# Attention by pairs of heads in the token mixer of a decoder layer: two column halves for the value product, feature-major output, probabilities divided on GpSimd

## The chip, the cores and the metric

The kernel runs on one core of a Trainium2 chip. The metric is the device time of one execution in microseconds (us), as the median over runs; lower is better. The profile and the trace come from one further execution.

## What is computed

One decoder layer on 512 tokens with D = 1024: a feed-forward block, a token mixer, a second feed-forward block and a gated per-layer embedding. The change lies in the mixer, which has two branches on the same input: a gated delta rule (8 heads of 64, chunks of 64 tokens, one triangular system per chunk and head) and sparse attention (8 heads of 64, the top 128 earlier keys of each query). Cut to what matters here:

```
def gated_delta_rule(q, k, v, g, beta):
    ...
    a_mat = jnp.where(strict, beta[..., :, None] * kk * decay, 0.0) + jnp.eye(C, dtype=jnp.float32)
    rhs = jnp.concatenate([v * beta[..., None], k * (beta * jnp.exp(gc))[..., None]], axis=-1)
    sol = lax.linalg.triangular_solve(a_mat, rhs, left_side=True, lower=True, unit_diagonal=True)
    ...

def dsa_attention(q, k, v, q_idx, k_idx, w_idx):
        ...
        _, sel = lax.top_k(score, top)
        valid = sel <= qpos[None, :, None]
        k_sel = gather(k, sel)
        v_sel = gather(v, sel)
        att = jnp.einsum("bqhd,bqkhd->bhqk", qb, k_sel).astype(jnp.float32) * (Dh ** -0.5)
        att = jnp.where(valid[:, None], att, -jnp.inf)
        prob = jax.nn.softmax(att, axis=-1).astype(v.dtype)
        return jnp.einsum("bhqk,bqkhd->bqhd", prob, v_sel)

def token_mixer(...):
    ...
    y_a = o_a.reshape(B, S, W_A) @ w_br_a
    ...
    o_b = dsa_attention(qb, kb, vb, qi, ki, w_i)
    y_b = o_b.reshape(B, S, W_B) @ w_br_b
    merged = jax.nn.sigmoid(g_a) * y_a + jax.nn.sigmoid(g_b) * y_b
    return merged @ w_out
```

## The kernel before

All large products take both operands as two exact parts and run three matmuls (lines 95 to 97). Weights are loaded in chunks of 128x2048 halves (`raw`), split by ACT (line 90) and DVE (line 91) ahead of use. The instructions are scheduled by the tile framework, which sets each engine's order from its own model of their times; inside an engine the order is fixed after that, and an instruction that waits holds back all behind it. PSUM has eight banks in two rings of four, `mmp` and `axp`.

**Attention.** There are no gathers: a bias tile per query tile `tt` (128 queries, S = 128 (tt + 1) keys) shuts out the keys that are not selected. 32 units (query tile, head) go through three steps, written one unit apart in the program. `att_soft`: one matmul of 64 rows gives the scores `pat` (line 705), DVE adds the bias and takes the minimum in one instruction (line 709, with a small read of the accumulator behind it), ACT takes the exponential and its sum (line 711), DVE the reciprocal (line 713). `att_tr`: the tile `at` is transposed 128 keys at a time into `ppt` (the helper of line 103) and copied to `pt` (line 725, DVE for heads 0 and 4, otherwise ACT). `att_pv`: per 128 keys a matmul with `pt` as weights and 64 columns of values moving gives `pob`, token-major (line 735); ACT writes it to `obt`, times the reciprocal of the sum (line 737). At the end 16 transposes `pobt` turn `obt` feature-major, and ACT and DVE make its parts `ob_hi` and `ob_lo` (lines 785, 786), which the branch's output product `pyb` uses.

**The delta rule beside it.** `chunk_blocks` gives the products k k and q k of four heads a step, times a decay tile `DT`: DMA, a select on POOL (line 638), subtraction on DVE, exponential on ACT, matmuls `pA`, and four products on DVE into `BT` and `KQs` (line 656). Its last three steps are written among the first units of the attention, behind units 2, 4 and 6, and at unit 7 `solve` follows: the diagonal blocks go out by DMA (`dgd`, line 661) and come back as `dz` (line 742). Then 31 steps of two DVE instructions each (lines 748 and 750) invert them in place. The result goes through memory again (`zd`, `dz`, `BT`, lines 752 to 758) and one DVE transpose makes `XC` (line 759). The 32x32 matmuls `pw` (line 820) need it, and so does the rest of the branch.

**What PE has besides.** `ptm` is the gate projection of the delta rule: 192 matmuls of 256 columns in the stretch looked at, which depend on neither the attention nor the solve. The tiles `at`, `DT` and the indexer's `rl` share a ring of three buffers, `pt` has two.

Of the kernel before, what the change touches and what calls it, by code (L numbers as in the profile page):

```python
# [7 lines left out]
F32 = mybir.dt.float32  # L8
# [7 lines left out]
T = 512  # L16
# [16 lines left out]
def layer_kernel(ctx, tc, x, pT, wf1, wo1, wfm, wsm, wtm, wbr, wout, wf2, wo2, wgate, wproj,  # L33
# [80 lines left out]
    def inv_rms(ss, half):  # L114
        """1/sqrt(mean + eps) from sums of squares over D, times 1/2 if half."""
# [7 lines left out]
    def first_u(tt, h, u, t):  # L123
        """make_u with the gain of FFN 1, which lies along the partitions."""
# [21 lines left out]
    def make_u(tt, h, gn, u, t):  # L146
        """u = rmsnorm(h) of one token tile, features on partitions, as two exact parts."""
# [70 lines left out]
    def start_tiles(tiles, u):  # L218
        """tiles: (weights, rows, evacuate), one half of the tokens after the other."""
# [316 lines left out]
    for tt in (3, 2, 1):  # L536
        S = 128 * (tt + 1)
        sc = tp.tile([128, S], F32, name=f"sc{tt}")
        for hd in range(8):
# [3 lines left out]
            rl = tp.tile([128, T], F32, name="rl", tag="at", bufs=3)  # L543
# [82 lines left out]
    def chunk_blocks():  # L626
        """Products k k and q k of one chunk of 128 tokens with the decay between two tokens, four heads a step."""
        for c in range(4):
# [6 lines left out]
            for h4 in range(2):  # L635
                DT = tp.tile([128, 4, 128], F32, name="DT", tag="at", bufs=3)
# [60 lines left out]
    units = [(tt, 2 * p + i) for p in range(4) for tt in (3, 0, 2, 1) for i in range(2)]  # L697
    ats, pts, pos, rss = {}, {}, {}, {}

    def att_soft(i):  # L700
        tt, hd = units[i]
        S = 128 * (tt + 1)
        b, pr = 64 * (hd % 2), hd // 2
        pa = axp("pat")
        PE.matmul(pa[:, :S], qbT[b:b + 64, pr, tt * 128:tt * 128 + 128], kbT[b:b + 64, pr, :S],  # L705
                  start=True, stop=True)
        at = tp.tile([128, T], F32, name="at", bufs=3)
        nm = sp.tile([128, 1], F32, name="nm", bufs=4)
        V.tensor_tensor_reduce(at[:, :S], pa[:, :S], bias[tt], 1.0, BIG, ALU.add, ALU.min, nm)
        sm1 = sp.tile([128, 1], F32, name="sm1", bufs=4)  # L710
        A.activation(at[:, :S], at[:, :S], AF.Exp, bias=nm, scale=-1.0, accum_out=sm1)
        rs = sp.tile([128, 1], F32, name="rs", bufs=6)
        V.reciprocal(rs, sm1)
        ats[i] = at
        rss[i] = rs

    def att_tr(i):
        tt, hd = units[i]
        S = 128 * (tt + 1)
        at = ats.pop(i)  # L720
        ppt = axp("ppt")
        for s_ in range(tt + 1):
            tr(ppt[:, s_ * 128:(s_ + 1) * 128], at[:, s_ * 128:(s_ + 1) * 128])
        pt = tp.tile([128, T], F32, name="pt", bufs=2)
        (A.copy if hd % 4 else V.tensor_copy)(pt[:, :S], ppt[:, :S])
        pts[i] = pt

    def att_pv(i):
        tt, hd = units[i]
        if hd % 2 == 0:  # L730
            pos[0] = mmp("pob")
        po, pt = pos[0], pts.pop(i)
        c = slice(64 * (hd % 2), 64 * (hd % 2) + 64)
        for s_ in range(tt + 1):
# [378 lines left out]
```

## Time and profile before

| what | value |
| --- | --- |
| median of 3 runs | 1319.71 us (1318.6 to 1321.0) |
| profiled execution, span of the trace | 1315.2 us |
| PE busy | 1291.6 us (98%) |
| DVE, ACT, POOL busy | 637.5, 469.0, 68.8 us |

The span is that of the trace's first to last instruction; the runs' times lie 4.5 us above it (1319.71 less 1315.2), and sums are made against the span and then carried to the median. Busy PE counts records; a float32 matmul of the attention leaves two records, a transpose one. Weight loads (PEld) run beside matmuls.

### The profile page before, as it was taken

To read this page: it belongs to the slowest core of one execution; us is meant where nothing else is said; L and a number is where in the kernel's file an instruction comes from. 1 tells how busy PE (TensorE), PEld (TensorE's weight loads), DVE (VectorE), ACT (ScalarE), POOL (GpSimd) and SP (SyncE) were. 2 spreads that over 40 slices of the span, in tenths; PEclk is the share of its full clock that TensorE was granted. 3 is DMA by queue.
4 is the path that set the end of the run, shared out by engine and by line. 5 is a ranking of instruction groups with operands and counts; after the bars stand their busy time and mean duration, and the time that the engine had idled before them with its cause. 6 is when DMAs were issued, how large, how long until landed. Compare 5 with 4: busy or idle time off the path is not lost.

```text
span 1315.2 us, 17630 instructions
## 1 busy us (share of the span) xinstructions
PE 1291.6 (98%) x7141; PEld 1095.4 (83%) x7141; DVE 637.5 (48%) x1088; ACT 469.0 (36%) x781; POOL 68.8 (5%) x71
## 2 busy tenths in 40 slices
PE   7999999999999999999999999989999999999997
PEld 6988888888889999887679888879888888888886
DVE  6233333322362699977685454563333333223555
ACT  6222222212252553445564223343222222212353
POOL 0000000000010000030001001220000000000000
PEclk9999999999999999999999999999999999999999
DMA  6233333333442223344305545522433333333331
GB/s 219 64 128 96 96 97 98 97 94 96 129 136 83 73 70 115 96 117 134 89 1 135 188 144 171 185 70 88 128 96 96 96 97 96 96 97 102 106 113 64
DMA packets 57777, 141.33 MB, mean 107 GB/s; under 512 B 17568, under 2 KB 20064, under 8 KB 57696
## 3 DMA queue, kind: packets, MB, share of 16 engines
q1 hardware_dynamic: 56688, 136.54, 34.0%
q10 hardware_dynamic: 1008, 3.67, 0.9%
q8 instruction: 56, 0.92, 0.3%
q14 instruction: 25, 0.20, 0.1%
HBM read 128.62 MB, written 11.57 MB: 107 GB/s over the span
## 4 chain that ended last, share of the span: by engine, by line
PE 88%; DMA 4%; DVE 4%; ACT 2%; POOL 1%; issue 1%; SPq 0%; POOLq 0%; DVEq 0%; ACTq 0%
PE pgu L95 11%; PE pgu L96 11%; PE pgu L97 11%; PE acc L95 6%; PE acc L97 6%; PE acc L96 6%; PE p L96 2%; PE p L97 2%; PE p L95 2%; PE ptm L97 2%; PE ptm L96 2%; PE ptm L95 2%; PE pg L95 2%; PE pg L97 2%; PE pg L96 2%; PE pat L705 2%
## 5 line engine op out<-in xcount | busy, mean ns | idle before, releaser
L91 DVE TENSOR_TENSOR wlo<-raw,whi 128x1024 fp32r<-128x1024 f32 x180 | 221.9, 1233 | 338.8 <-ACT whi L90 333.2
L90 ACT CAST whi<-raw 128x1024 fp32r<-128x1024 f32 x180 | 189.3, 1052 | 526.2 <-PE pgu L96 161.6
L96 PE MATMUL pgu<-ulo,whi 128*128 128x512 f32 x624 | 242.8, 389 | 0.0
L95 PE MATMUL pgu<-uhi,whi 128*128 128x512 f32 x624 | 242.8, 389 | 0.0
L97 PE MATMUL pgu<-uhi,wlo 128*128 128x512 f32 x624 | 242.8, 389 | 0.0
L97 PEld LDWEIGHTS pgu<-uhi,wlo 128*128 128x128 f32 x624 | 117.1, 188 | 24.5
L95 PEld LDWEIGHTS pgu<-uhi,whi 128*128 128x128 f32 x624 | 117.1, 188 | 24.2
L96 PEld LDWEIGHTS pgu<-ulo,whi 128*128 128x128 f32 x624 | 117.1, 188 | 24.1
L96 PE MATMUL acc<-wlo,hid 128*128 128x512 f32 x288 | 113.9, 395 | 0.0
L95 PE MATMUL acc<-whi,hid 128*128 128x512 f32 x288 | 113.9, 395 | 0.0
L97 PE MATMUL acc<-whi,hid 128*128 128x512 f32 x288 | 113.3, 396 | 0.0
L257 DVE TENSOR_TENSOR gt<-pgu,gt 128x512 f32<-128x512 f32 x39 | 27.0, 692 | 132.1 <-PE pgu L97 132.1
L96 PE MATMUL ptm<-wlo,uhi 128*128 128x256 f32 x256 | 72.1, 284 | 0.0
L97 PE MATMUL ptm<-whi,ulo 128*128 128x256 f32 x256 | 72.0, 284 | 0.0
L95 PE MATMUL ptm<-whi,uhi 128*128 128x256 f32 x256 | 71.7, 284 | 0.0
L96 PEld LDWEIGHTS acc<-wlo,hid 128*128 128x128 f32 x288 | 54.1, 188 | 13.1
L97 PEld LDWEIGHTS acc<-whi,hid 128*128 128x128 f32 x288 | 54.1, 188 | 13.1
L95 PEld LDWEIGHTS acc<-whi,hid 128*128 128x128 f32 x288 | 54.1, 188 | 13.0
L77 POOL TENSOR_TENSOR rinv<-ms,mhalf 128x1 f32<-128x1 f32 x32 | 19.0, 594 | 838.2 <-DVE ms L118 835.3
L97 PEld LDWEIGHTS ptm<-whi,ulo 128*128 128x128 f32 x256 | 48.9, 191 | 0.2
L96 PEld LDWEIGHTS ptm<-wlo,uhi 128*128 128x128 f32 x256 | 48.9, 191 | 0.1
L95 PEld LDWEIGHTS ptm<-whi,uhi 128*128 128x128 f32 x256 | 48.5, 191 | 0.2
(388 smaller groups left out, 2329.4 us busy)
## 6 DMA issues: line engine op xcount, KB each, us to landing
raw<-wf SPq DMA_DIRECT2D x88, 512.0 KB, 3.6
raw<-wo SPq DMA_DIRECT2D x44, 512.0 KB, 3.5
raw<-wfm SPq DMA_DIRECT2D x28, 512.0 KB, 3.7
raw<-wtm SPq DMA_DIRECT2D x20, 512.0 KB, 3.6
gd<-gst SPq DMA_DIRECT2D x16, 256.0 KB, 2.1
raw<-wbr SPq DMA_DIRECT2D x8, 512.0 KB, 3.8
grl<-gd SPq DMA_DIRECT2D x16, 256.0 KB, 3.1
raw<-wout SPq DMA_DIRECT2D x8, 512.0 KB, 4.1
```

The costliest lines, as they stand in the source:

```text
L77: G.tensor_tensor(out_, in_, e, op=ALU.pow)
L90: A.copy(hi[:, :n], raw[:, :n])
L91: (eng or V).tensor_sub(lo[:, :n], raw[:, :n], hi[:, :n].bitcast(F32))
L95: PE.matmul(ps, l[0], r[0], start=start, stop=False)
L96: PE.matmul(ps, l[0], r[1], start=False, stop=False)
L97: PE.matmul(ps, l[1], r[0], start=False, stop=stop)
L257: V.tensor_tensor(t[:, n], ps[:, n], t[:, n], op=ALU.mult)
L705: PE.matmul(pa[:, :S], qbT[b:b + 64, pr, tt * 128:tt * 128 + 128], kbT[b:b + 64, pr, :S], start=True, stop=True)
```

## The change

The units become 16 pairs (two heads of one row pair, one query tile). The two score matmuls of a pair are issued one behind the other in the two row halves of the array. After the reciprocal, POOL multiplies `at` by it in place (line 717 of the changed file), so that the transposes take normalized probabilities. The value product has the values as weights, 64 columns of the array for each head of the pair, and `pt` moving, so `pob` comes out feature-major, one bank for a pair's four query tiles. One ACT instruction per four pairs writes `obt` (line 743). The 16 transposes `pobt` are gone; `ob_hi` and `ob_lo` are made from `obt` in SBUF (lines 786 and 787). The ring of `at`, `DT` and `rl` has five buffers, that of `pt` four. The steps of `chunk_blocks` and the solve are written behind pairs 1, 2 and 3. Lines of the changed file are some two to seven higher than before.

```diff
-            rl = tp.tile([128, T], F32, name="rl", tag="at", bufs=3)
+            rl = tp.tile([128, T], F32, name="rl", tag="at", bufs=5)
...
-                DT = tp.tile([128, 4, 128], F32, name="DT", tag="at", bufs=3)
+                DT = tp.tile([128, 4, 128], F32, name="DT", tag="at", bufs=5)
...
-    units = [(tt, 2 * p + i) for p in range(4) for tt in (3, 0, 2, 1) for i in range(2)]
+    pairs = [(p, tt) for p in range(4) for tt in (3, 0, 2, 1)]
...
+    def att_soft(g):
+        p, tt = pairs[g]
         S = 128 * (tt + 1)
+        pa = [axp("pat") for _ in range(2)]
+        for i in range(2):
+            hb = slice(64 * i, 64 * i + 64)
+            PE.matmul(pa[i][:, :S], qbT[hb, p, tt * 128:tt * 128 + 128], kbT[hb, p, :S], start=True, stop=True)
+        ats[g] = []
+        for i in range(2):
+            at = tp.tile([128, T], F32, name="at", bufs=5)
...
+            V.reciprocal(rs, sm1)
+            G.tensor_scalar(at[:, :S], at[:, :S], rs, None, op0=ALU.mult)
+            ats[g].append(at)
...
+            pt = tp.tile([128, T], F32, name="pt", bufs=4)
+            (A.copy if (2 * p + i) % 4 else V.tensor_copy)(pt[:, :S], ppt[:, :S])
...
+    def att_pv(g):
+        p, tt = pairs[g]
+        if g % 4 == 0:
+            pos[0] = mmp("pob")
+        po, pt = pos[0], pts.pop(g)
         for s_ in range(tt + 1):
-            PE.matmul(po[:, c], pt[:, s_ * 128:(s_ + 1) * 128], vb[:, s_, hd * 64:(hd + 1) * 64],
-                      start=s_ == 0, stop=s_ == tt)
-        A.activation(obt[:, tt, hd * 64:hd * 64 + 64], po[:, c], AF.Copy, scale=rss.pop(i))
+            for i in range(2):
+                PE.matmul(po[64 * i:64 * i + 64, tt * 128:tt * 128 + 128], vb[:, s_, p * 128 + 64 * i:p * 128 + 64 * i + 64],
+                          pt[i][:, s_ * 128:(s_ + 1) * 128], start=s_ == 0, stop=s_ == tt, tile_position=(0, 64 * i))
+        if g % 4 == 3:
+            A.activation(obt[:, p, :], po, AF.Copy, scale=0.5)
...
-    for i in range(len(units) + 3):
-        if i < len(units):
-            att_soft(i)
-        if i in (2, 4, 6):
+    for g in range(len(pairs) + 2):
+        if g < len(pairs):
+            att_soft(g)
+        if g in (1, 2, 3):
             next(blocks, None)
-        if i == 7:
+        if g == 3:
             for _ in blocks:
                 pass
             ZC, XC, Z = solve()
...
-    for tt in range(4):
-        tk = slice(tt * 128, tt * 128 + 128)
-        pt = axp("pobt")
-        for pr in range(4):
-            tr(pt[:, pr * 128:pr * 128 + 128], obt[:, tt, pr * 128:pr * 128 + 128])
-        pt = pt.rearrange("p (a b) -> p a b", b=128)
-        A.activation(ob_hi[:, :, tk], pt, AF.Copy, scale=0.5)
-        V.scalar_tensor_tensor(ob_lo[:, :, tk], pt, 0.5, ob_hi[:, :, tk].bitcast(F32), op0=ALU.mult, op1=ALU.subtract)
+    for p in range(4):
+        A.copy(ob_hi[:, p], obt[:, p])
+        V.tensor_sub(ob_lo[:, p], obt[:, p], ob_hi[:, p].bitcast(F32))
```

What the change moves on the engines is read from the order of the instructions in the two programs. First DVE around the end of the solve (lines 748 and 750, in the changed file 754 and 756), before:

```order
L786 SCALAR_TENSOR_TENSOR ob<-pobt,ob 128x4x128
L748 TENSOR_TENSOR ztmp<-dz 128x60
L750 TENSOR_TENSOR dz<-dz,ztmp 128x30x2
L748 TENSOR_TENSOR ztmp<-dz 128x31
L750 TENSOR_TENSOR dz<-dz,ztmp 128x31
L91 TENSOR_TENSOR wlo<-raw,whi 128x1024 x2
L759 STREAM_TRANSPOSE dz<-dz 128x1024
```

and of the change (L712 is the add and minimum of a score tile, L716 the reciprocal, L787 makes `ob_lo`):

```order
L756 TENSOR_TENSOR dz<-dz,ztmp 128x30x2
L712 ISA at,nm<-pat,sc_3293 128x384
L712 ISA nm 128x1
L754 TENSOR_TENSOR ztmp<-dz 128x31
L712 ISA at,nm<-pat,sc_3293 128x384
L712 ISA nm 128x1
L756 TENSOR_TENSOR dz<-dz,ztmp 128x31
L716 RECIPROCAL rs<-sm_5880 128x1
L716 RECIPROCAL rs<-sm_5888 128x1
L712 ISA at,nm<-pat,sc_3345 128x256
L712 ISA nm 128x1
L787 TENSOR_TENSOR ob<-obt,ob 128x512 x2
```

Before, the last score tile is taken well ahead of the solve's last steps, and all four instructions that make `ob_lo` stand inside the solve. Now the score tiles of the last two pairs stand at and behind the solve's last step, and `ob_lo` behind that. Between the first and the last instruction of the solve stand 17 instructions on score tiles in both programs, and the same four copies of `pt`.

Next PE at the first `pw`, before:

```order
L97 MATMUL ptm<-whi,ulo 128x256
L820 MATMUL pw<-dz,BT 32x32 x64
L95 MATMUL pyb<-ob,whi 128x512
L96 MATMUL pyb<-ob,whi 128x512
L97 MATMUL pyb<-ob,wlo 128x512
```

and of the change:

```order
L95 MATMUL ptm<-whi,uhi 128x256
L96 MATMUL ptm<-wlo,uhi 128x256
L97 MATMUL ptm<-whi,ulo 128x256
L821 MATMUL pw<-dz,BT 32x32 x5
L740 MATMUL pob<-pt,vb 64x128 x3
L821 MATMUL pw<-dz,BT 32x32 x48
L95 MATMUL ptm<-whi,uhi 128x256
```

Before, all 192 `ptm` stand ahead of the first `pw`. Now 72 stand ahead of it and 120 behind, most of them before the first `pyb`. Of the 72, 14 stand ahead of the last pair's score matmuls, 10 between these and the transposes of the last but one pair, and 48 behind those, with 10 transposes and 7 value matmuls of the last two pairs.

Last POOL, of the change (before, only the select of `DT` stood here; the multiplications are line 717):

```order
L812 MEMSET S_5981 128x512
L717 TENSOR_SCALAR at<-at,rs 128x512 x2
L717 TENSOR_SCALAR at<-at,rs 128x128 x2
L638 AFFINE_SELECT DT<-DT 128x512
L717 TENSOR_SCALAR at<-at,rs 128x384 x2
L638 AFFINE_SELECT DT<-DT 128x512
L717 TENSOR_SCALAR at<-at,rs 128x256 x2
L638 AFFINE_SELECT DT<-DT 128x512
L717 TENSOR_SCALAR at<-at,rs 128x512 x2
```

The 32 multiplications come one for each score tile, the first eight between the selects of the last three steps of `chunk_blocks`; 16 of them belong to pairs whose score tiles stand inside the solve on DVE.

## Rows read from the trace of the kernel before

**Rows 1.** The page: engines, granted clock in 40 slices, shares of the chain.
```profile
PE 1291.6 (98%) x7141; PEld 1095.4 (83%) x7141; DVE 637.5 (48%) x1088; ACT 469.0 (36%) x781; POOL 68.8 (5%) x71
...
PEclk9999999999999999999999999999999999999999
...
PE 88%; DMA 4%; DVE 4%; ACT 2%; POOL 1%; issue 1%; SPq 0%; POOLq 0%; DVEq 0%; ACTq 0%
```
**Rows 2.** Windows: busy us and instructions of PE, PEld, DVE, ACT, POOL.
```profile
652.20:691.84 39.64, 39.59 (x258) 29.95 (x257) 32.67 (x122) 25.23 (x78) 0.00 (x0) 1.00 0.00 1
691.84:707.96 16.12, 16.12 (x139) 15.99 (x139) 4.01 (x4) 4.95 (x8) 3.85 (x3) 1.00 0.85 164
707.96:760.00 52.04, 52.04 (x596) 45.18 (x596) 30.83 (x57) 17.51 (x32) 3.17 (x2) 1.00 0.55 179
```
**Rows 3.** Groups of PE by form, 600 to 708: busy us, mean ns.
```profile
L735 PE MATMUL pob<-vb,pt 128*128 128x64 f32 x160 | 22.1, 276 | 0.0
```
**Rows 4.** Timeline of PE: start, duration, line, records; at 609, 675, 681, 707.
```profile
609.21 1.13 PE L705 MATMUL pat<-hz 64*128 64x512 f32 x4
...
675.71 0.91 PE L705 MATMUL pat<-hz 64*128 64x384 f32 x2
...
677.44 1.33 PE L735 MATMUL pob<-vb,pt 128*128 128x64 f32 x10
...
681.54 0.93 PE L103 MATMUL pobt<-cst,obt 128*128 128x128 f32 x7
...
707.08 0.28 PE L95 MATMUL ptm<-whi,uhi 128*128 128x256 f32 x1
707.20 0.28 PE L96 MATMUL ptm<-wlo,uhi 128*128 128x256 f32 x1
...
707.89 2.21 PE L820 MATMUL pw<-dz,BT 32*32 32x32 f32 x128
```
**Rows 5.** Groups of DVE, 652.20 to 691.84: busy us, mean ns, idle before, releaser.
```profile
L750 DVE TENSOR_TENSOR dz<-dz,ztmp 128x31 f32<-128x31 f32 (+15 forms) x31 | 10.5, 339 | 0.4
L748 DVE TENSOR_TENSOR ztmp<-dz 128x31 f32<-128x31 f32 (+15 forms) x31 | 10.5, 338 | 1.6 <-DMA dz<-dgd 1.2
L709 DVE CUSTOM_DVE_ANT_0 at<-pat,sc 128x256 f32<-128x256 f32 (+2 forms) x13 | 7.1, 546 | 2.7 <-PE pat L705 2.5
L713 DVE RECIPROCAL rs<-sm 128x1 f32<-128x1 f32 x18 | 2.9, 158 | 0.6 <-ACT at L711 0.4
L786 DVE SCALAR_TENSOR_TENSOR ob<-pobt,ob 128x512 fp32r<-128x512 f32 x4 | 2.8, 689 | 1.1 <-ACT ob L785 0.9
```
**Rows 6.** Timelines of DVE and SP at the solve's start and end.
```profile
644.87 2.58 SPq L661 DMA_DIRECT2D dgd<-BT  x4
...
652.21 0.19 DVE L748 TENSOR_TENSOR ztmp<-dz 128x31 f32<-128x31 f32 x1 [1.20 <-DMA dz<-dgd]
...
691.62 0.22 DVE L750 TENSOR_TENSOR dz<-dz,ztmp 128x31 f32<-128x31 f32 x1
...
700.39 1.25 DVE L759 STREAM_TRANSPOSE dz<-dz 128x1024 f32<-128x1024 f32 x1 [1.33 <-DMA dz<-zd]
```
**Rows 7.** Groups of POOL, 600 to 708 us.
```profile
L933 POOL TENSOR_TENSOR zs<-zs,prm 128x512 f32<-128x512 f32 x3 | 3.8, 1294 | 61.0 <-ACT zs L931 61.0
L638 POOL TENSOR_SCALAR_AFFINE_SELECT DT<-DT 128x512 f32<-128x512 f32 x5 | 3.2, 638 | 43.8 <-DMA DT<-rowd 43.8
```
**Rows 8.** Timelines of DVE and POOL near 817 us, and of DVE at 707 us.
```profile
817.95 2.32 DVE L91 TENSOR_TENSOR wlo<-raw,whi 128x1024 fp32r<-128x1024 f32 x1
...
817.51 1.68 POOL L975 TENSOR_TENSOR grl<-grl,ybm 128x512 f32<-128x512 f32 x1 [1.27 <-DVE grl L974]
...
707.64 1.23 DVE L91 TENSOR_TENSOR wlo<-raw,whi 128x1024 fp32r<-128x1024 f32 x1 [6.00 <-ACT whi L90]
```

**Rows 9.** Timeline of PE at the start of the span.
```profile
15.09 0.41 PE L96 MATMUL p<-ulo,whi 128*128 128x256 f32 x1
15.30 0.41 PE L97 MATMUL p<-uhi,wlo 128*128 128x256 f32 x1
```

More of the change, by code (lines that the diff above doesn't have):

```diff
@@ L696, in layer_kernel @@
     obt = mx.tile([128, 4, T], F32, name="obt", tag="oa")
-    units = [(tt, 2 * p + i) for p in range(4) for tt in (3, 0, 2, 1) for i in range(2)]
-    ats, pts, pos, rss = {}, {}, {}, {}
-    def att_soft(i):
-        tt, hd = units[i]
+    pairs = [(p, tt) for p in range(4) for tt in (3, 0, 2, 1)]
+    ats, pts, pos = {}, {}, {}
+    def att_soft(g):
+        p, tt = pairs[g]
         S = 128 * (tt + 1)
[L703 to L715, printed above, removed]
@@ L717, in att_tr @@
-    def att_tr(i):
-        tt, hd = units[i]
-        S = 128 * (tt + 1)
-        at = ats.pop(i)
-        ppt = axp("ppt")
-        for s_ in range(tt + 1):
[L723 to L734, printed above, removed]
-            PE.matmul(po[:, c], pt[:, s_ * 128:(s_ + 1) * 128], vb[:, s_, hd * 64:(hd + 1) * 64],
-                      start=s_ == 0, stop=s_ == tt)
-        A.activation(obt[:, tt, hd * 64:hd * 64 + 64], po[:, c], AF.Copy, scale=rss.pop(i))
+        pa = [axp("pat") for _ in range(2)]
@@ new lines, in att_soft @@
+        for i in range(2):
[4 more added lines that the diff above has]
+            at = tp.tile([128, T], F32, name="at", bufs=5)
+            nm = sp.tile([128, 1], F32, name="nm", bufs=4)
+            V.tensor_tensor_reduce(at[:, :S], pa[i][:, :S], bias[tt], 1.0, BIG, ALU.add, ALU.min, nm)
+            sm1 = sp.tile([128, 1], F32, name="sm1", bufs=4)
+            A.activation(at[:, :S], at[:, :S], AF.Exp, bias=nm, scale=-1.0, accum_out=sm1)
+            rs = sp.tile([128, 1], F32, name="rs", bufs=6)
+            V.reciprocal(rs, sm1)
+            G.tensor_scalar(at[:, :S], at[:, :S], rs, None, op0=ALU.mult)
+            ats[g].append(at)
@@ new lines, in att_tr @@
+    def att_tr(g):
+        p, tt = pairs[g]
+        S = 128 * (tt + 1)
+        pts[g] = []
+        for i, at in enumerate(ats.pop(g)):
+            ppt = axp("ppt")
+            for s_ in range(tt + 1):
+                tr(ppt[:, s_ * 128:(s_ + 1) * 128], at[:, s_ * 128:(s_ + 1) * 128])
+            pt = tp.tile([128, T], F32, name="pt", bufs=4)
+            (A.copy if (2 * p + i) % 4 else V.tensor_copy)(pt[:, :S], ppt[:, :S])
+            pts[g].append(pt)
+    def att_pv(g):
+        p, tt = pairs[g]
+        if g % 4 == 0:
+            pos[0] = mmp("pob")
+        po, pt = pos[0], pts.pop(g)
+        for s_ in range(tt + 1):
+            for i in range(2):
[3 more added lines that the diff above has]
+            A.activation(obt[:, p, :], po, AF.Copy, scale=0.5)
@@ L770, in layer_kernel @@
             ZC, XC, Z = solve()
[L771 removed]
+        if g == 0:
             conv_tr(*late.pop())
[L773 to L776 removed]
+        if 0 <= g - 1 < len(pairs):
+            att_tr(g - 1)
+        if 0 <= g - 2 < len(pairs):
+            att_pv(g - 2)
     ob = hp.tile([128, 2, 4, T], F32R, name="ob", tag="hz")
     ob_hi, ob_lo = ob[:, 0], ob[:, 1]
[L779 to L786 removed]
+    for p in range(4):
+        A.copy(ob_hi[:, p], obt[:, p])
+        V.tensor_sub(ob_lo[:, p], obt[:, p], ob_hi[:, p].bitcast(F32))
     att_pool.close()
```

7 lines of the change are left out of this document (1 added, 6 removed).

## The prediction

> **What bounds the kernel now.** I read the page first: PE is busy 98% of the span, 88% of the chain that ended last runs on it, and its granted clock is full in every slice [rows 1]. Taken alone that says: what leaves PE leaves the time. Then the windows by stage, since a share is an average. In the stretch of the triangular solve, 652.20 to 691.84, PE is busy 39.59 of 39.64 us, but DVE is busy 32.67 of them [rows 2]: the second engine is 7 us behind the first. Behind it, up to the first `pw` at 707.9, PE is full of work that needs no solve, and from there to 760 it is full again (52.04 of 52.04) [rows 2]. So before, PE covers everything that DVE and the memory round trip of the solve take. The question is how much of the saving in PE this cover survives.
>
> **What PE saves.** Durations are read from a group and from single records [rows 3, 4]. (a) Scores: one 384-column matmul alone lasts 0.91 us, and the four records at 609.21, two 512-column matmuls that already stand in the two row halves, last 1.13 us together. A pair thus costs about what one costs. 32 matmuls of mean size 320, at some 0.75 us (0.91 scaled down by columns), are 24 us; half of that is 12. From this I take 3 off, since the pair keeps its change of array shape and some were neighbours already: 9. (b) Values: 160 records [rows 3], ten of them in 1.33 us, less the last one's tail (0.27, the mean of one) 0.11 each: 17.7 us. The new ones have twice the columns, half the weights' width and the same count. If the two column halves run together, 160 records take the place of 80: 9 us saved; if not, 0. No row shows two column halves at once. The nearest is `pw`, 128 records of 32x32 in 2.21 us, 0.017 each, which must overlap; so I take 9 and keep 0 as the end. (c) 16 `pobt` transposes at 0.11 to 0.13 (seven in 0.93): 2. Together S = 20, bounds 11 and 20.
>
> [...]
>
> **What DVE has to do, and when.** The solve's first instruction waits for `dz`, 7.34 us behind the issue of `dgd` (644.87 to 652.21) [rows 6]. That chain is DMA and `BT`'s products, not PE, so PE's saving does not pull it forward; deeper buffers and the earlier place of the steps may, a little. I take 651, bounds 647 and 652. From then the solve is 31 + 31 instructions, 10.5 + 10.5 us. In both programs 17 score tiles, 16 to 18 reciprocals and four copies stand between its ends. What leaves this stretch is the four `ob_lo` (2.8 us) and two reciprocals (0.3) [rows 5]: 32.67 - 3.1 = 29.6 us of DVE work. Before, DVE also stood idle 7 us there, mostly for `pat` (2.5) and `dz` (1.2) [rows 2, 5]. PE has less to do between two `pat` now, but a score tile's path is longer by the multiplication, and DVE meets the tiles in a fixed order: 3.6 us, half of 7, with bounds 0 and 7. End of the solve: 651 + 29.6 + 3.6 = 684.2, against 691.84.
>
> PE has not enough to fill that: its 39.6 us there lose most of S, and the filler that stood behind the attention (`ptm`) is largely not moved into it. Only 14 `ptm` stand ahead of the last pair's scores. So PE will wait for DVE inside the attention, which it never did before.
>
> **Behind the solve.** The end of the solve to `XC` took 9.8 us (691.84 to 700.39 + 1.25) [rows 6]. I keep that. In the meantime PE does 48 `ptm` at 0.12 [rows 4] (5.8 us), ten transposes, seven value matmuls and their changes of shape (2.5 us), so `pw` starts about 9.8 us behind the solve. The three value matmuls between the `pw` cost 0.3. Behind the first `pw` PE still has 120 `ptm`, 14.4 us, which before lay ahead of it; all else there is the same and PE is full to the end of the stretch [rows 2]. So the end moves by: end of solve + 9.8 + 0.3 + 14.4 - 707.9, which is zero for a solve that ends at 683.4. For 684.2 it is +0.8 us. Nearly all of S is gone.
>
> **The multiplications on POOL.** 32 are added, 16 beside the solve. No row shows one. The nearest is the select with one input, 0.638 us at 512 columns; a two-input operation takes 1.294 [rows 7]. I take the select's price, scaled to 0.64, 0.54, 0.45 and 0.36 for the four sizes: 4 x 1.99 = 8.0 us of POOL. It would be off the path if DVE did not feel it. It does: at 817.51 POOL starts a 512-column add on SBUF, and DVE's `wlo`, 1.23 us alone, takes 2.32; POOL's add takes 1.68 in place of 1.29 [rows 8]. The solve's instructions have SBUF alone in and out, as `wlo` has. Before, POOL is idle in the whole solve (0.00) [rows 2]. So DVE loses up to 8.0 us; some fall on DVE's waits or on score tiles read from PSUM. I take 5.5; bounds 0 and 8 (16 at the two-input price). The solve then ends at 689.7 and the time grows by 0.8 + 5.5 = 6.3 us.
>
> [...]
>
> Other edits: ACT loses 32 evictions and gets four wide ones; it is busy 25.23 of 39.64 there [rows 2], so nothing. The deeper rings only remove waits. The smaller DMA scratch and the docstrings cost nothing by what the profile shows; SP issues the same transfers.
>
> **Sum.** Against the span of 1315.2: 1315.2 + 6.3 = 1321.5. The runs' median lies 4.5 above the span, so 1326.0.
>
> **Rivals.** (A) PE stays the bound and S is kept: 1319.7 - 20 = 1300, or 1309 without concurrent column halves. For it speaks the page's 98%; against it that the solve would have to end near 664 (684 - 20) with 29.6 us of DVE work from 651 on. A part of it remains if `dz` comes at 647 and DVE hardly waits: the solve ends at 677, and the time is 1319.7 - 6.4 = 1313. (B) POOL and DVE don't meet in the solve, as these instructions are short: +0.8, 1320.5. For it: no row shows a one-input POOL operation against a DVE instruction. (C) The multiplication costs the two-input price, 1.29 at 512: 16 us of POOL beside the solve, DVE loses 11 to 16, and each pair's path grows by as much again: +12 to +17, 1332 to 1336. This is decided by the price of one 512-column multiplication: near 0.6 or near 1.3. [...] (E) The column halves don't run together: the change then does not do what it says. Its 9 us lie mostly beside DVE's stretch; behind the solve only ten records are left, 1 us: 1327.
>
> [...]
>
> **Chances.** Forecast with E: 0.42 (1322.5 to 1330). B: 0.23, spread around its 1320.5. A, whole or in part: 0.19. C: 0.09, D: 0.07. A measurement of this kernel can tell about 0.2% (2.6 us) from no change: faster is below 1317.1, slower above 1322.3. A gives 0.19 faster, and B's lower end 0.06; B gives 0.14 same and a little slower, the forecast 0.03 same. So 0.25, 0.17, 0.58. Range: from the middle of A's partial case and its full one, 1308, to C's upper end, 1335, which leaves out most of A's full case and little else. The forecast's own range is 1322 to 1330.
>
> **What would show it.** Right: PE busy falls well below 39.6 in the solve's stretch and its idle time is released by DVE on score tiles; the first solve step at 650 to 652; its instructions' mean rises above 338 ns where POOL runs, and POOL's multiplications are about 0.64 at 512; `pw` some 10 us behind the last step; PE full afterwards. Wrong: `dz` before 648, solve steps at 338 ns beside POOL, or `pw` before 693. The column halves show in the spacing of `pob`: 0.055 a record, or 0.11.

## The result and the profile after

The changed kernel takes 1333.07 us (median of 4 runs, 1332.55 to 1333.7) beside 1319.49 for the kernel before: 13.6 us slower, a ratio of 1.0099 with an interval of 1.0073 to 1.0124. The prediction was 1326 with a range of 1308 to 1335: the direction and the place were right, the size was half of what came, and the part that was forecast as dearest was not the part that cost. The time lies beyond the forecast's own range of 1322 to 1330 and inside the stated one only because that reaches up to rival C.

The page of the profile after (engines, granted clock in 40 slices, shares of the chain), beside [rows 1]:

```profile
PE 1291.5 (97%) x7125; PEld 1090.4 (82%) x7125; DVE 641.4 (48%) x1088; ACT 461.0 (35%) x751; POOL 105.5 (8%) x103
...
PEclk9999999999999999999799999999999999999999
...
PE 88%; DVE 5%; DMA 3%; ACT 2%; POOL 1%; issue 1%; SPq 0%; DVEq 0%; POOLq 0%; ACTq 0%
```

PE's busy time is the same as before to 0.1 us, although work left it (20 us by the prediction's sum, about 15 by the run without a division below). That is not a contradiction: one slice of the granted clock now shows a 7, and the same work took longer where it was low. Four transposes take 0.66 us at 630.8, at a granted clock of 1.00, and 1.11 at 632.3, at 0.50; the window that holds both has 0.59 on average:

```profile
630.79 0.66 PE L103 MATMUL ppt<-cst,at 128*128 128x128 f32 x4 [1.65 <-POOL at L717]
632.34 1.11 PE L103 MATMUL ppt<-cst,at 128*128 128x128 f32 x4 [0.89 <-POOL at L717]
...
630.00:640.00 10.00, 7.06 (x32) 4.30 (x34) 5.16 (x19) 3.62 (x12) 6.42 (x7) 0.59 0.25 65
```

The page averages all of this away; the windows of the attention show it (columns as in [rows 2], the granted clock behind POOL):

```profile
624.45:656.83 32.38, 26.32 (x177) 17.13 (x173) 17.77 (x64) 14.81 (x40) 14.62 (x15) 0.79 0.35 91
656.83:690.73 33.90, 25.23 (x141) 14.43 (x140) 31.57 (x116) 14.96 (x45) 18.07 (x16) 0.85 0.00 1
690.73:704.97 14.24, 14.24 (x115) 11.89 (x114) 4.39 (x12) 5.54 (x16) 4.75 (x4) 1.00 0.69 112
704.97:760.00 55.03, 55.03 (x654) 49.59 (x654) 30.81 (x55) 22.45 (x41) 7.04 (x5) 1.00 0.40 127
```

From the first score matmul to the solve's end PE is idle for 6.1 + 8.7 = 14.7 us, where it was full before (27.60 of 27.60 us from 624.6 to 652.2, and [rows 2]), and it runs at a granted clock of 0.79 and 0.85 on average, and at 0.50 from 632.3 to 636.0. From the solve's end on it is full again. What PE waits for stands in its list of waits (us in total, times, the longest), where POOL is the largest entry, and in the view of the tile `ppt`, the transposes: idle time before the instructions on it (us, times) until

```profile
PE ppt L103 <- POOL at L717: 8.4, 8, 2.1
```

```profile
  POOL at L717: 20.0, 19
  PE ppt L103: 17.7, 13
  issue: 2.6, 9
  POOL DT L638: 1.6, 3
```

The line of POOL counts 8.4 us of PE and 11.6 of its weight loads, which lie beside each other; the line below it is the copies to `pt` that wait for the transposes. So 8.4 of PE's 14.7 idle us end with a product of POOL, and the other entries of its list are 2.5 us and less. And the multiplications are dearer than any row before had shown (groups of POOL, 600 to 725 us; the last is the select that gave the forecast's price):

```profile
L717 POOL TENSOR_SCALAR at<-at,rs 128x512 f32<-128x512 f32 x8 | 12.5, 1574 | 26.7 <-DVE rs L716 23.8 <-PE ppt L103 2.9
L717 POOL TENSOR_SCALAR at<-at,rs 128x384 f32<-128x384 f32 x8 | 10.1, 1277 | 14.8 <-DVE rs L716 12.3 <-PE pat L707 2.6
L717 POOL TENSOR_SCALAR at<-at,rs 128x256 f32<-128x256 f32 x8 | 8.2, 1030 | 4.0 <-DVE rs L716 4.0
...
L717 POOL TENSOR_SCALAR at<-at,rs 128x128 f32<-128x128 f32 x8 | 4.9, 625 | 0.7 <-PE ppt L103 0.7
L638 POOL TENSOR_SCALAR_AFFINE_SELECT DT<-DT 128x512 f32<-128x512 f32 x3 | 1.9, 634 | 3.0 <-PE ppt L103 3.0
```

1.57 us at 512 columns, and 35.7 us in all, where the forecast had 0.64 and 16. The points on the solve's way, beside [rows 6] (timelines of DVE, POOL, PE):

```profile
633.40 0.63 POOL L638 TENSOR_SCALAR_AFFINE_SELECT DT<-DT 128x512 f32<-128x512 f32 x1
...
645.45 0.64 POOL L638 TENSOR_SCALAR_AFFINE_SELECT DT<-DT 128x512 f32<-128x512 f32 x1 [2.98 <-PE ppt L103]
...
656.83 0.19 DVE L754 TENSOR_TENSOR ztmp<-dz 128x31 f32<-128x31 f32 x1 [2.22 <-DMA dz<-dgd]
...
690.51 0.21 DVE L756 TENSOR_TENSOR dz<-dz,ztmp 128x31 f32<-128x31 f32 x1
699.28 1.25 DVE L765 STREAM_TRANSPOSE dz<-dz 128x1024 f32<-128x1024 f32 x1 [2.58 <-DMA dz<-zd]
...
692.97 0.70 PE L707 MATMUL pat<-hz 64*128 64x256 f32 x4
...
704.97 0.37 PE L821 MATMUL pw<-dz,BT 32*32 32x32 f32 x10
```

`dz` comes 4.6 us later than before, the solve still ends 1.1 us earlier, and `XC` is ready at 700.5. But `pw` starts only at 705.0: the last pair's scores were taken at 693.0, and what hangs on them stands ahead of `pw`. With the 120 `ptm` behind it, the recurrence starts 11.4 us late (first `pvn` matmul 742.81, before 731.46). Another 4 us of this one execution come up behind the mixer, where the granted clock is 0.95 to 0.97 between 840 and 930 us (before 1.00); their cause is open. The two spans differ by 15.5 us and the medians by 13.6, so some 2 of these 4 us belong to the two executions that were profiled and not to the kernels.

### The profile page after: what moved, and what is told of

Its sections match the earlier page's. It is cut to its first block, busy times and chain, and to the rows that moved or that the text cites. A ratio compares the mean times of both kernels' runs of the same rounds, so it can differ in the third digit from the quotient of the medians.

```text
span 1330.7 us, 17639 instructions
## 1 busy us (share of the span) xinstructions
PE 1291.5 (97%) x7125; PEld 1090.4 (82%) x7125; DVE 641.4 (48%) x1088; ACT 461.0 (35%) x751; POOL 105.5 (8%) x103
## 4 chain that ended last, share of the span: by engine, by line
PE 88%; DVE 5%; DMA 3%; ACT 2%; POOL 1%; issue 1%; SPq 0%; DVEq 0%; POOLq 0%; ACTq 0%
PE pgu L97 11%; PE pgu L96 11%; PE pgu L95 11%; PE acc L95 7%; PE acc L97 7%; PE acc L96 7%; PE p L96 3%; PE p L95 3%; PE p L97 3%; PE ptm L95 2%; PE ptm L97 2%; PE ptm L96 2%; PE pg L95 2%; PE pg L96 2%; PE pg L97 2%; PE pc L96 2%
## 5 line engine op out<-in xcount | busy, mean ns | idle before, releaser
L97 PEld LDWEIGHTS pgu<-uhi,wlo 128*128 128x128 f32 x624 | 117.1, 188 | 24.2
L95 PEld LDWEIGHTS pgu<-uhi,whi 128*128 128x128 f32 x624 | 117.1, 188 | 24.2
```

The lines of the kernel that those rows point to most:

```text
L95: PE.matmul(ps, l[0], r[0], start=start, stop=False)
L97: PE.matmul(ps, l[1], r[0], start=False, stop=stop)
```

## The experiments

All times are set beside runs of the kernel before on the same chip in the same session (medians 1317.6 to 1320.3), and the ratios are to those. Two theories stood against each other at the start. **P**: POOL's division costs the time. **S** and **O**: DVE's solve, or the order that the scheduler drew, would cost it in any case. The scheduler orders the whole stretch anew for each kernel, so a run may differ from the changed kernel in more than its edit. "Port" is my name in the expectations for what DVE's instructions lose beside POOL's: the solve's take 23.6 us in the changed kernel, 21.0 before. What the two engines share there is shown by no run. In every run below all 192 `ptm` stand ahead of the first `pw`, as in the kernel before; the changed kernel alone has 120 of them behind it.

**No division at all.**

```diff
-            G.tensor_scalar(at[:, :S], at[:, :S], rs, None, op0=ALU.mult)
```

> The changed kernel without the multiplication by the reciprocal (the output is not divided by the sums; nothing else is left out). The scheduler then puts all 192 ptm ahead of pw again and ob_lo back into the solve. Theory P (the division on POOL costs the time: its price on the path of each pair, the DT select queued behind it, its port): PE has no long waits in the attention, dz comes at 650 to 652, the solve ends at 684 to 687, pw starts at 694 to 697, and the time is 1306 to 1311. Rival S (DVE's solve bounds in any case and eats the saving): the solve ends near 690, the time is 1316 to 1322. Rival K (PE's clock falls because the pairs leave PE idle anyway): granted clock below 0.9 in 652 to 690 and 1313 to 1318.

Measured: 1314.1 us, ratio 0.9972 (0.9953 to 0.9990). So P holds for the loss: without the division the change gains 4 us. But 4 is little, and the time lies above the 1306 to 1311 that I gave for P. It lies in K's range, without K's sign: the granted clock in the solve is 1.00. The windows to the solve's start, to its end, and to `pw`:

```profile
623.07:650.04 26.97, 25.25 (x189) 16.66 (x186) 19.20 (x73) 17.12 (x48) 1.90 (x3) 0.94 0.39 109
650.04:689.84 39.80, 39.80 (x314) 30.79 (x313) 33.45 (x121) 22.49 (x61) 0.00 (x0) 1.00 0.05 13
689.84:703.42 13.58, 13.47 (x85) 11.75 (x84) 2.53 (x3) 3.52 (x6) 5.40 (x4) 1.00 0.81 153
```

PE is nearly full before `dz` and full from there, `ptm` ends at 696.0 (before 707.7), so PE is 12 us ahead. The solve, though, ends at 689.84 against 691.84, and `pw` cannot start before 703.4. Behind it, from 703.4 to 730, PE is busy only 24.2 of 26.6 us at a clock of 0.81. That part of theory S is right: the solve and what hangs on it let through a third of what PE saves. But the solve is not alone in this. From its end to `XC` it takes 13.5 us here, 9.8 before, with two weight transfers (`raw`) now issued just ahead of the solve's way through memory; SP's issues, here and before:

```profile
687.10 1.65 SPq L84 DMA_DIRECT2D raw<-wbr  x2
689.86 0.33 SPq L757 DMA_DIRECT2D zd<-dz  x1
696.55 2.31 SPq L760 DMA_DIRECT2D dz<-zd  x4
```

```profile
691.87 0.34 SPq L752 DMA_DIRECT2D zd<-dz  x1
694.54 2.32 SPq L755 DMA_DIRECT2D dz<-zd  x4
```

The way back can be issued 6.7 us behind the way out, before 2.7. So `XC` is ready 1.7 us later than before, although the solve ended 2.0 us earlier. In the next run the two transfers go out 6.6 us ahead of it, and the same way takes 9.5 us. The run with a select and the first run with more lead have the same two transfers there, and 13.7 and 13.4 us.

**POOL does the same work, but nobody waits for it.**

```diff
-            G.tensor_scalar(at[:, :S], at[:, :S], rs, None, op0=ALU.mult)
+            jk = tp.tile([128, T], F32, name="jk", bufs=2)
+            G.tensor_scalar(jk[:, :S], at[:, :S], rs, None, op0=ALU.mult)
```

> As the changed kernel, but POOL writes its product into a tile that nobody reads (the output is not divided by the sums). POOL does the same work beside DVE and DT's selects still queue behind it; only PE no longer waits for the product. Theory P in its form 'path': the waits of the transposes on POOL were the cost: 1307 to 1313. Form 'queue and port': dz still comes at 655 to 657 and the solve's instructions stay 6 to 18% longer than before: 1316 to 1322.

Measured: 1314.2 us, ratio 0.9963 (0.9952 to 0.9975), the same as without POOL, 1 us above the range for the path and 2 below that for "queue and port". The groups of POOL and, within the solve, of DVE:

```profile
L718 POOL TENSOR_SCALAR jk<-at,rs 128x512 f32<-128x512 f32 x8 | 13.2, 1662 | 21.3 <-DVE rs L716 20.1 <-DVE dz L757 1.2
```

```profile
L755 DVE TENSOR_TENSOR ztmp<-dz 128x31 f32<-128x31 f32 (+15 forms) x31 | 13.1, 421 | 0.6
L757 DVE TENSOR_TENSOR dz<-dz,ztmp 128x31 f32<-128x31 f32 (+15 forms) x31 | 12.4, 401 | 0.5
```

This is the run that says most. POOL is as busy as in the changed kernel, DVE's instructions are longer beside it (the solve's take 25.5 us in place of 21.0), the selects of `DT` queue behind nearly as many multiplications (3, 6 and 8 of them in place of 4, 6 and 8), and yet `dz` comes at 651.0 and the time is that of no division. The equal time is in part luck: the solve ends 3.6 us later than without POOL (693.4), less than the 4.5 us by which its instructions are longer, but its way through memory takes 9.5 us and not 13.5, so `XC` is ready at 703.0 in place of 703.3. So the longer instructions and the queue can make a few microseconds, not the 19 between this run and the changed kernel. What is left is that in the changed kernel something waits for the product, with what follows from that: PE's idle time, its lower granted clock, and the other order that the scheduler draws for it. This run takes away all three at once.

**The same place at a lower price.**

```diff
+            G.affine_select(at[:, :S], at[:, :S], pattern=[[1, S]], compare_op=ALU.is_ge, fill=0.0, base=0, channel_multiplier=0)
```

(in place of the multiplication)

> As the changed kernel, with a one-input select that lets every element pass in place of the multiplication (the output is not divided by the sums): same place on POOL and on the path, at 0.64 us for 512 columns in place of 1.57. Theory P: the time follows the price: the product's delay per pair falls by some 60%, dz at 652 to 653, and the time is 1309 to 1316. Forecast's own reading (0.64 on POOL costs as much as written in the prediction): 1326. Rival S: 1318 to 1322.

Measured: 1317.8 us, ratio 1.0001 (0.9986 to 1.0015); 2 us above what P had said, at the edge of S, and 8 below the 1326 of the forecast, though POOL has the forecast's price here. The solve's instructions take 22.7 us in place of 21.0: at this price DVE loses 1.7 us beside POOL, not the 5.5 of the sum. POOL's group at 512 columns, and the idle time before the transposes that POOL ended (us, times): 5.6 against 20.0.

```profile
L717 POOL TENSOR_SCALAR_AFFINE_SELECT at<-at 128x512 f32<-128x512 f32 x8 | 5.1, 640 | 26.7 <-ACT at L714 26.6
```

```profile
  POOL at L717: 5.6, 13
```

**The division as a two-input instruction.**

```diff
+            G.tensor_tensor(at[:, :S], at[:, :S], rs.to_broadcast([128, S]), op=ALU.mult)
```

(in place of the multiplication)

> The changed kernel with the division on POOL written as a two-input multiplication by the broadcast reciprocal: the same result, another price, and the scheduler then orders the rest as it does without the division (all ptm ahead of pw, ob_lo inside the solve). If the price on POOL decides: about 1.3 us at 512 columns lies between the 0.64 of the select run (1317.8) and the 1.57 of the changed kernel (1333.1): 1324 to 1330. If the order decides: 1315 to 1320 in spite of the price. Port: a two-input POOL operation should lengthen the solve's instructions at least as much as the 13% of the changed kernel.

Measured: 1319.5 us, ratio 1.0006 (0.9989 to 1.0022). Both of my numbers were off: the form costs 1.06 us at 512 columns, not 1.3, and the time fell below the range that I gave for the price. It lies in the one that I gave for the order, 1315 to 1320, and the order is again not that of the changed kernel; since the form is cheaper than I assumed, the run does not tell the two apart. The profile is of its slowest execution (1323.3 us).

```profile
L717 POOL TENSOR_TENSOR at<-at,rs 128x512 f32<-128x512 f32 x8 | 8.4, 1058 | 25.9 <-DVE rs L716 21.4 <-DVE dz L756 1.9 <-PE pat L707 1.6
```

```profile
  POOL at L717: 14.2, 23
```

What the expectation says of the port came: the solve's instructions take 13.7 + 13.6 = 27.3 us, the most of all runs, and again this is not where the time goes. With the runs above this makes a row: POOL at 0 (or aside), 0.64, 1.06 and 1.57 us for 512 columns; transposes wait 0, 5.6, 14.2 and 20.0 us for it; the time is 1314, 1318, 1319.5 and 1333. The last step is steeper than the others, and the last kernel differs from the other three in its order too. The price orders the runs better than the waits do: two runs below that also pay 1.57 wait only 12.0 and 4.9 us and take 1328.5 and 1329.2.

**Is the order behind `pw` part of it?** The first `pw` may not pass what is ahead of it in the program:

```diff
-                PE.matmul(pw[p0 + 32:p0 + 64, i * 32:i * 32 + 32], ...)
+                w_ = PE.matmul(pw[p0 + 32:p0 + 64, i * 32:i * 32 + 32], ...)
+                if c == i == p0 == 0:
+                    tc.keep_in_program_order(w_)
```

> The changed kernel with one edit: the first pw may not pass what stands ahead of it on PE in the program, so all 192 ptm come before it again; up to there every engine's order is that of the changed kernel. If the 120 ptm behind pw are part of the loss (rival O): the time falls by 5 us or more, below 1328. If they are only work that PE does later, since PE is full from the solve's end on in both orders: pw starts 14 us later, at 719, and the time is the changed kernel's, 1331 to 1335.

Measured: 1334.5 us, ratio 1.0127 (1.0094 to 1.0160): no better.

```profile
720.72 0.28 PE L97 MATMUL ptm<-whi,ulo 128*128 128x256 f32 x1
720.93 0.76 PE L821 MATMUL pw<-dz,BT 32*32 32x32 f32 x36
```

`pw` starts at 720.9 rather than 705.0, and all else follows. PE has the same work left when the attention ends, in whichever order; the 120 `ptm` are a sign of the delay and no cause.

**Without column halves.** Both heads' values as weights, for each head a bank of its own of which half is used; POOL's division stays.

```diff
...
-                PE.matmul(po[64 * i:64 * i + 64, tt * 128:tt * 128 + 128], vb[:, s_, p * 128 + 64 * i:p * 128 + 64 * i + 64],
-                          pt[i][:, s_ * 128:(s_ + 1) * 128], start=s_ == 0, stop=s_ == tt, tile_position=(0, 64 * i))
+                PE.matmul(po[i][:, tt * 128:tt * 128 + 128], vb[:, s_, p * 128:p * 128 + 128],
+                          pt[i][:, s_ * 128:(s_ + 1) * 128], start=s_ == 0, stop=s_ == tt)
...
```

> The changed kernel without column halves: 128 value columns as weights for each head, two banks, half of each used; POOL's division stays. If column halves run together only here and there or PE's time is hidden: same as the changed kernel, 1331 to 1336. If PE's time counts: value matmuls take 0.11 us a record in place of 0.055, 9 us more, 1338 to 1343. Rival O (the order made it slow: the scheduler now puts all ptm ahead of pw): 1320 to 1328 in spite of the dearer matmuls.

Measured: 1328.5 us, ratio 1.0079 (1.0056 to 1.0102): faster than the changed kernel, with dearer matmuls, and 0.5 us above the range for rival O. The records, here and in the changed kernel:

```profile
656.05 1.06 PE L740 MATMUL pob<-pt,vb 128*128 128x128 f32 x8
```

```profile
691.95 1.09 PE L740 MATMUL pob<-pt,vb 128*64 128x128 f32 x14
```

Less the tail of one (0.27), that is 0.11 us a record with the whole array and 0.06 with two halves: the column halves do run together. Yet their gain of some 8 us is not seen in the time; PE has 11.4 us of idle time there, from 624 to the solve's end. This kernel has POOL's full price and another order (all `ptm` ahead of `pw`, the last score tiles inside the solve on DVE). It lies 10 us above the kernel before, with no more work on PE than that has, so the price costs in that order too (POOL ends 12.0 us of idle time before the transposes); the 5 us by which it is faster than the changed kernel, in spite of its dearer matmuls, may be the order inside the attention, which no run isolates.

**The division on ACT.**

```diff
+            A.activation(at[:, :S], at[:, :S], AF.Copy, scale=rs)
```

(in place of the multiplication)

> The changed kernel with the division on ACT (a copy scaled by the reciprocal), the same result. [...] Theory P: close to the run without the division plus what the select cost: 1315 to 1320. If ACT becomes the engine that is waited for: 1321 to 1327.

Measured: 1317.7 us, ratio 0.9993 (0.9971 to 1.0014), as P had it; ACT takes 0.71 us at 512 columns, and the solve's instructions are back at 339 ns.

**Pairs of scores only.** Values token-major and scaled at ACT's eviction, with the 16 transposes, as before.

```diff
-        if g % 4 == 0:
-            pos[0] = mmp("pob")
-        po, pt = pos[0], pts.pop(g)
+        po, pt = mmp("pob"), pts.pop(g)
...
+                PE.matmul(po[:, c], pt[i][:, s_ * 128:(s_ + 1) * 128], vb[:, s_, p * 128 + 64 * i:p * 128 + 64 * i + 64],
+                          start=s_ == 0, stop=s_ == tt)
+            A.activation(obt[:, tt, p * 128 + 64 * i:p * 128 + 64 * i + 64], po[:, c], AF.Copy, scale=rss.pop((g, i)))
```

> Only the pairing is kept: score matmuls in pairs, pairs in the program's order, deeper rings; the value product stays token-major with the scaling in ACT's eviction as before, with the 16 transposes; nothing on POOL. The full computation. If pairing is what the change gains and the division what it loses: PE saves about 9 us, of which DVE's solve lets through some 3 to 5: 1313 to 1317. If the column halves and the feature-major output carried the gain of the run without a division: 1318 to 1321.

Measured: 1320.1 us, ratio 0.9994 (0.9961 to 1.0027): no gain, and in the range for the case that column halves and feature-major output carried the gain. The windows from 624 us speak for another cause:

```profile
624.00:640.00 16.00, 13.95 (x88) 8.76 (x87) 10.72 (x38) 9.48 (x23) 1.27 (x2) 0.83 0.44 123
640.00:660.00 20.00, 20.00 (x102) 16.70 (x103) 9.05 (x36) 8.99 (x30) 0.64 (x1) 0.63 0.21 57
```

No multiplication is on POOL here, and PE is busy for all of 640 to 660, but at a granted clock of 0.63. It had waited 2 us in the window before, for the first pairs' softmax. The kernel before takes its first two score tiles at 609.2, among the gate tiles; in all kernels with pairs the first stands at 623 to 627, with nothing of that kind to cover it. I had not seen that in the order. The eight executions bear it out: the fastest, 1312.3 us, has a mean granted clock of 0.997, the slowest, 1324.3, one of 0.986. So this run does not tell what pairing is worth at full clock.

**One pair more of lead.** Transposes two pairs behind the scores, values three, seven buffers; POOL's multiplication unchanged.

```diff
...
-        if 0 <= g - 1 < len(pairs):
-            att_tr(g - 1)
-        if 0 <= g - 2 < len(pairs):
-            att_pv(g - 2)
+        if 0 <= g - 2 < len(pairs):
+            att_tr(g - 2)
+        if 0 <= g - 3 < len(pairs):
+            att_pv(g - 3)
```

> The changed kernel with the same multiplication on POOL (1.57 us at 512 columns, the same 35 us in all), but one pair more between a pair's scores and its transposes: transposes two pairs behind the scores, values three, seven buffers in the ring and ten for the reciprocals. If the latency of the product on the path is the cost (theory P, path): PE no longer waits on POOL, the granted clock stays near full, and the time falls to 1314 to 1319 although POOL and its port are as busy as before. If POOL's throughput or the port is the cost: 1325 to 1333.

Measured: 1329.2 us, ratio 1.0102 (1.0044 to 1.0159), against the expectation of theory P, in the range for POOL's throughput or the port. The waits did go: POOL ends 4.9 us of idle time before the transposes, not 20.0. The time did not. PE's first transposes, and windows:

```profile
632.77 0.66 PE L103 MATMUL ppt<-cst,at 128*128 128x128 f32 x4 [0.45 <-POOL at L717]
634.32 0.93 PE L103 MATMUL ppt<-cst,at 128*128 128x128 f32 x4 [0.89 <-POOL at L717]
...
630.00:640.00 10.00, 8.65 (x40) 4.78 (x38) 6.43 (x29) 5.76 (x19) 8.86 (x10) 0.73 0.48 147
640.00:650.00 10.00, 9.19 (x49) 7.07 (x47) 5.67 (x22) 3.50 (x11) 6.12 (x6) 0.50 0.16 39
650.00:660.00 10.00, 9.94 (x41) 5.57 (x42) 3.85 (x16) 4.39 (x13) 2.49 (x2) 0.58 0.26 67
660.00:670.00 10.00, 10.00 (x67) 5.42 (x66) 8.12 (x35) 6.25 (x21) 7.67 (x7) 1.00 0.00 1
```

After two waits of 0.45 and 0.89 us for POOL among the first pairs, PE's granted clock is 0.50 and 0.58 for twenty microseconds in which it is busy 19.1 of 20. The products for `BT` fall into that stretch, so `dz` comes at 661.7 and the solve ends at 704.5, 13 us later than before. Here the loss runs through the clock and the solve. That the first products queue on POOL is part of it: POOL works without a gap from 631.1 to 641.4. What DVE loses beside POOL is not: in the next run the solve's instructions are longer still (26.6 us against 22.9 here), and the time is 9 us less.

**The same lead with the cheaper POOL form, and with ACT.** The edits are those above, together.

> Both levers: one pair more of lead and the cheaper two-input form on POOL (1.06 us at 512). Theory P: little left for PE to wait for; the bound is DVE's solve and what follows it, as in the run without a division: 1313 to 1317. If the lead itself costs (later values, more buffers held): 1318 to 1322.

> One pair more of lead with the division on ACT (0.6 to 0.7 us at 512), nothing on POOL. The solve's instructions should be back at 338 ns. Theory P: 1312 to 1316, the best of all that divide. If ACT's queue (exponentials, copies, divisions) is what PE waits for: 1317 to 1321.

Measured: 1320.6 us, ratio 1.0018 (0.9999 to 1.0037), and 1316.5 us, ratio 0.9990 (0.9978 to 1.0002). Both lie above what P had said (1313 to 1317 and 1312 to 1316), the first in the range for a lead that costs by itself. With the same lead, the same 512 columns at 1.57, 1.06 and 0.71 us give 1329, 1321 and 1316: the price counts at this lead too. The run on ACT is the best that divides, and no different from the kernel before by its interval.

**The division taken off that path.** The reciprocals are spread along the tokens by PE, and the result is divided once per four pairs.

```diff
...
+        for i in range(2):
+            PE.matmul(prs[64 * i:64 * i + 64, tt * 128:tt * 128 + 128], rss.pop((g, i)).to_broadcast([128, 64]), ident,
+                      start=True, stop=True, tile_position=(0, 64 * i))
...
-            A.activation(obt[:, p, :], po, AF.Copy, scale=0.5)
+            A.activation(obt[:, p, :], prs, AF.Copy, scale=0.5)
+            V.tensor_tensor(obt[:, p, :], po, obt[:, p, :], op=ALU.mult)
```

> The full computation with pairs, column halves and feature-major output, the division taken off the path to the transposes: for each head one more matmul (the reciprocals as weights, spread over 64 columns, the identity moving) writes the reciprocals along the tokens into a second bank, ACT copies that once per four pairs, and one DVE multiplication per four pairs divides. 32 matmuls of 128 columns more (64 records, 3.5 to 7 us of PE), DVE 4 x 0.7 us more, ACT 4 copies as before, nothing on POOL. Theory P (what costs is that PE waits for a divided tile): like the run without a division plus DVE's 2.8 us: 1314 to 1318, a little below the kernel before. If every form of division costs what the others cost: 1317 to 1321, no different from before.

Measured: 1318.4 us, ratio 0.9993 (0.9972 to 1.0015): no different from before, and in the range for the case that every form of division costs alike. The windows to the solve's start and to its end:

```profile
624.00:653.80 29.80, 28.31 (x206) 19.01 (x202) 19.52 (x69) 16.07 (x43) 1.90 (x3) 0.89 0.34 100
653.80:696.33 42.53, 42.53 (x323) 30.25 (x324) 33.80 (x128) 23.26 (x65) 0.00 (x0) 1.00 0.01 2
```

PE is full in the solve and POOL out of it, and the solve ends at 696.3, 4.5 us later than before: it starts 1.6 us later, and DVE waits 3.4 us in it for `pob`, ahead of three of the new multiplications (2.1 us). No version that computes the whole layer came out clearly faster than the kernel before.

## Why the prediction was right, and where it was off

**Right: the bound behind PE.** The prediction said that PE's saving would be swallowed, since DVE's solve stands 7 us behind PE, and that PE would wait inside the attention for the first time. Both came, the second for another reason: it was to be DVE on score tiles that PE waits for, and it was POOL. The solve ended at 690.7 (forecast 689.7). The run without a division shows the swallowing alone: of 12 us by which PE is ahead at the end of `ptm`, 4 reach the end. The 20 us of the sum were too many: these 12, with the 1.7 us that PE idles ahead of `dz` there and at most 1.6 that the clock of 0.94 takes, make about 15 (an estimate from that run's windows). The 3 us that the sum took off for changes of array shape are shown by no run as a sum; one change shows in the spacing, 0.21 us from a `ptm` to a `pob` (703.85 to 704.06 in the changed kernel) beside 0.12 from `ptm` to `ptm`.

**Right by compensation: the solve's end.** Its parts were off in both directions. `dz`, forecast at 651 with bounds 647 and 652, came at 656.8, because the first multiplications kept PE waiting and its granted clock fell (0.59 from 630 to 640), and the last select of `DT` started only at 645.4, having waited 3.0 us for the release by `ppt`; before:

```profile
641.42 0.64 POOL L638 TENSOR_SCALAR_AFFINE_SELECT DT<-DT 128x512 f32<-128x512 f32 x1 [4.40 <-DMA DT<-rowd]
```

The run with POOL aside, where PE does not wait, has `dz` at 651.0 behind nearly as many multiplications. The stretch from `dz` to the solve's end was forecast at 33.2 + 5.5 us and took 33.9: 23.6 us for the solve's own instructions (before 21.0, so DVE lost 2.6 beside POOL, not 5.5), 8.0 of other work, and 2.3 idle, not 3.6. That late start and short stretch cancel to within 1 us is luck.

**Where the 13.6 us stand.** Put into the prediction's own formula, a solve that ends at 690.7 gives 690.7 + 9.8 + 0.3 + 14.4 - 707.9 = +7.3 us. What the sum lacks is the 4.4 us by which `pw` comes later than 9.8 behind the solve, and some 2 us behind the mixer.

**Wrong: the price of the multiplication.** "I take the select's price", 0.64 us at 512 columns, with 1.29 as the other end. It took 1.57, beyond both ends: a one-input operation with a scalar per partition was dearer than the two-input rows, and the two-input form of the same multiplication cost 1.06. This is the term that was mis-sized; the sum over 16 was 8.0 and is 18.0 us (4 x 4.51).

**Wrong: the way it acts.** "It would be off the path if DVE did not feel it." It was on the path of the transposes: the 3.6 us of waits that the sum allowed were DVE's for scores, and none were PE's for the product. POOL aside shows the difference: with 4.5 us lost by DVE beside POOL, the time is that of no division, though 4 us less on the way through memory helped it. Nor was DVE's loss right at the price that was assumed: with the select in the same place it is 1.7 us, and the time is 1317.8, not 1326. Had the price been as assumed, the forecast would have been 8 us too high, as far as that run's order goes. The meeting at 817 us [rows 8], 1.1 us lost beside an add of 1.29, did not carry over: in the solve 18 us of POOL's multiplications took 2.6 us from DVE's instructions, and 17.6 us, with 2.6 of another product on POOL, took 4.5 when aside. The score tiles, which DVE reads from PSUM, lost nothing there: the one of 512 columns at 666.93 lies wholly beside a multiplication (666.88, 1.56 us) and takes 0.69 us, and the mean is 681 ns (before 691).

**Wrong: the end of the solve to `pw`.** Forecast 9.8 us, measured 14.2. `XC` was ready after 9.8 as said, but PE came late to the last pair, as its idle time lay ahead of it. The 14.4 us of `ptm` behind `pw` were counted rightly.

**The rivals.** C, the dearer multiplication (1332 to 1336), is the case that came, with a chance of 0.09 in the text; its condition, a price of 1.3 or more at 512 columns, was met, though its way through DVE was not. D, a lower granted clock, with a chance of 0.07 in the text, came as a part: the granted clock of 0.79 and 0.85 in the changed kernel, and in two other runs 0.50 to 0.63 over twenty microseconds in which PE was almost always busy (19.1 and 20.0). In these three traces the low clock follows waits of PE: 1.65 and 0.89 us in the changed kernel, 0.45 and 0.89 with one pair more of lead, 2.05 in all with pairs of scores only. Not every wait brings it: from 840 to 900 us PE of the kernel before idles 3.8 us at a granted clock of 1.00. B, no meeting of POOL and DVE in the solve, fell in its premise, since the solve's instructions are 13% longer; with the select in the multiplication's place the time is nearer to its 1320.5 than to the forecast. E fell: the column halves run together, at 0.06 us a record. A fell with the run without a division.

**What stays open.** How the 13.6 us divide among waiting for the product, PE's lower granted clock that follows it, and the order inside the attention that the scheduler drew for the dear multiplication. An estimate from the windows: up to the solve's end PE idles 14.7 us and loses at most 11.9 to the granted clock (0.21 of 32.4 us and 0.15 of 33.9); less the 15 saved that is some 12, beside the 11.4 by which the recurrence starts late. It does not say how much of the idle time the order makes. The order behind `pw` is excluded; the price is shown at two leads: the four runs in which a product at 1.57 us is read take 1328 to 1335, all others 1314 to 1321; the run with whole arrays leaves some 5 us or more for the rest of the order. A run with the changed kernel's order and a cheap multiplication was not made.

## What to carry to other kernels

An operation that is moved to an idle engine is not free because the engine is idle: ask who waits for its result, and price it by its exact form, since on POOL the same multiplication cost 1.57 us with a scalar per partition and 1.06 us with a broadcast tensor. A saving on the busiest engine is worth only what the second engine lets through (here 4 of 12 us); look for the stretch where the second is closest. And a short wait of PE can cost more than its length: with one pair more of lead the granted clock was 0.50 and 0.58 for twenty microseconds behind waits of 0.45 and 0.89 us. Read the granted clock behind each wait, since not every wait brings that (1.00 in the kernel before, with 3.8 us idle from 840 to 900).

## What the runs showed of the hardware that was not expected

POOL multiplied 512 float32 columns in 1.57 us with a scalar per partition, in 1.06 us with the same scalar as a broadcast second input, and passed them through a select in 0.64 us. POOL's work beside DVE's two-input instructions on SBUF lengthened these by 13% in the changed kernel (23.6 against 21.0 us) and by 30% (27.3) with the two-input form, that is by 2.6 us beside 18 us of POOL's multiplications in the changed kernel, where the single meeting at 817 us [rows 8] had suggested 1.1 us beside an instruction of 1.29. After waits of 0.45 and 0.89 us (more lead) or 2.05 us (pairs of scores only) PE's granted clock was 0.50 and 0.58, or 0.63, over the twenty microseconds from 640 on, while it was busy 19.1 and 20.0 of them. Two weight transfers issued just ahead of the solve's small round trip through memory went with 13.5 us from the solve's end to `XC`, against 9.8 without them.
